# Where the prompt's heads stand in the attention loop, and how a pair's heads are taken out

## The chip, the cores and the metric

The kernel runs on one core of one Trainium2 chip. The metric is device time in microseconds (us) of one execution of the whole program, a decoder step of four layers. The attention of layer 2 is one stage of it, and the change is in that stage alone.

## What is computed

Layer 2 is stick-breaking attention with 16 heads of 64, over two kinds of rows: a prompt of 272 rows, and 8 sequences of 4 new rows each, with 1024 earlier keys and values per sequence that lie in pages of 128 in a pool.

```python
z = jnp.einsum('bqhd,bshd->bhqs', qblk, kf) * scale + bf
mask = (k_pos[None, :] < pblk[:, None])[None, None]
log_not = jnp.where(mask, jax.nn.log_sigmoid(-z), 0.0)
between = lax.cumsum(log_not, axis=3, reverse=True) - log_not
wts = jnp.where(mask, jnp.exp(jax.nn.log_sigmoid(z) + between), 0.0)
return jnp.einsum('bhqs,bshd->bqhd', wts, vf)
...
mp = op.reshape(bp, lp, D_MODEL) @ attn_w_o[j]
ms = os_.reshape(bs, ls, D_MODEL) @ attn_w_o[j]
```

Both results go through one output projection with `attn_w_o`, prompt rows and sequence rows side by side (304 columns).

## The kernel before

The 8 sequences are worked in 4 pairs `p`, and the pages of a pair in slots: slot `sl` holds 4 key pages, or 4 value pages. One loop over `u` (L1562 on) does a quarter of a slot a step:

- `keys_t(u+2)` turns 8 blocks of 128x128 of the key pages round on TensorE (L1332), and ScalarE and VectorE copy them out (L1337, L1338);
- `keys(u)` multiplies them with the queries into the scores `zs` (L1351): 4 matmuls, each on its own 32 columns of the array;
- `values(u-24)`, every second step, multiplies two value pages with the weights into `av` (L1415): 4 matmuls, again each on its own 32 columns, two for each page; the first of a pair also takes the new rows (L1413);
- `scores`, `weights` and `weights_t` make a pair's weights in between, and `heads(p)` (L1424 on) turns a pair's finished `av` round (L1428), then takes the heads out, ScalarE the rounded part into `ohi` (L1443) and VectorE the rest into `olo` (L1444).

Key steps run up to `u` = 63, value steps from `u` = 24 to `u` = 86, so the steps after 63 have values alone.

The prompt's own attention is cut into pieces of two heads: `prompt_z` (scores, L1477 and L1478), `prompt_c` (running sums, L1491 to L1495) and `prompt_o` (times the values, L1506 to L1508), in the order z1, o0, c1, z2 and so on, 23 pieces within the loop. The table `at` names the step `u` behind which each one is written.

A page is loaded by one DMA of 512 KB that SyncE issues into one of 13 buffers (8 `raw`, 5 `rawx`), in a fixed order: key and value pages in turn, then the 8 blocks of `attn_w_o`. A load waits until the page that held the buffer is used up (`key_done`). Blocks of `attn_w_o` are then split into a rounded part (`hi`, L208, ScalarE) and a rest (`lo`, L211, VectorE).

The code is not run in the order in which it is written: the framework that builds the program sets one fixed order for each engine beforehand, by times of its own, and each engine then works strictly through its list. The lists are what is compared below.

Of the kernel before, what the change touches and what calls it, by code (L numbers as in the profile page):

```python
# [9 lines left out]
F32 = mybir.dt.float32  # L10
F32R = mybir.dt.float32r
I32 = mybir.dt.int32
AF = mybir.ActivationFunctionType
ALU = mybir.AluOpType
# [46 lines left out]
class Trunk:  # L61
# [1211 lines left out]
    def attention(self, l):  # L1273
        nc, I, O = self.nc, self.I, self.O
        v = nc.vector
        with self.tc.tile_pool(name="att", bufs=1) as ap:
# [146 lines left out]
            def heads(p):  # L1423

                am = va.pop(p)
                po = self.bank()
                for c in range(4):
                    nc.tensor.transpose(po[:, c * 128:(c + 1) * 128], am[:, c * 128:(c + 1) * 128], self.ident)  # L1428
                cs = slice(NP + 8 * p, NP + 8 * p + 8)
                for h in range(2):  # L1430
                    hs = slice(h * 64, h * 64 + 64)
                    for i in range(2):

                        o = 32 * i + 4 * h
                        for c0, c1 in ((0, 3), (3, 4)):
                            if c0 == 0:
                                pv = po[hs, o:o + 408].rearrange("p (c x) -> p c x", x=136)[:, :, 0:128].rearrange("p c (s x) -> p c s x", x=64)[:, :, :, 0:4]
                            else:

                                pv = po[hs, 384:512].rearrange("p (s x) -> p s x", x=64)[:, :, 24 + o:28 + o].unsqueeze(1)  # L1440
                            hi = ohi[hs, 4 * i + c0:4 * i + c1, cs].rearrange("p c (s q) -> p c s q", q=4)
                            lo = olo[hs, 4 * i + c0:4 * i + c1, cs].rearrange("p c (s q) -> p c s q", q=4)
                            nc.scalar.activation(hi, pv, AF.Copy)  # L1443
                            v.tensor_tensor(lo, pv, hi.bitcast(F32), ALU.subtract)  # L1444

            z2 = ap.tile([80, 16, 16], F32, name="z2")[64:80]
            L2 = ap.tile([80, 16, 16], F32, name="L2")[64:80]
# [117 lines left out]
            ohi = self.up.tile([128, ND, N], F32R, tag="uhi", name="ohi")  # L1565
            olo = self.up.tile([128, ND, N], F32R, tag="ulo", name="olo")
            prompt = [(f, d - lag) for d in range(10) for f, lag in ((prompt_o, 2), (prompt_c, 1), (prompt_z, 0)) if 0 <= d - lag < 8]

            at = [22 + k * 2 for k in range(23)]
            del prompt[0]  # L1570
            for u in range(4 * (16 + LAG) + 3):
                if u + LEAD < 64:
                    keys_t(u + LEAD)
                if u < 64:
                    keys(u)
                p, r = divmod(u, 16)
                if p < 4:
                    if r == 8:
                        scores(p, 0)
                    if r == 10 and p < 3:  # L1580
                        queries(p + 1)
                if 0 < p < 5:
                    if r == 0:
                        scores(p - 1, 1)
                        weights(p - 1)
                    if r == 5:
                        weights_t(p - 1)
                c = u - 4 * LAG
                if c >= 16 and c % 16 == 1:
                    heads(c // 16 - 1)  # L1590
                if 0 <= c < 64:
                    values(c)
                if u == 4 * (16 + LAG) - 6:
                    self.split_blocks(self.index[("o", l), 0, 1])
                while at and at[0] == u:
                    f, d = prompt.pop(0)
                    f(d)
                    del at[0]
# [117 lines left out]
```

## Time and profile before

| what | us |
|---|---|
| median of 3 runs | 1662.12 (1660.5 to 1664.52) |
| profiled execution | 1663.34 |
| its span | 1661.6 |
| TensorE busy | 1510.3 |
| VectorE busy | 1206.0 |
| ScalarE busy | 829.3 |
| GpSimd busy | 546.8 |

Times in the rows are counted from the start of the span. The loop of the attention lies between about 780 and 993 us. In a row of the timeline the first number is the start and the second how long the group took from first start to last end; since matmuls overlap, what a group costs is read from its start to the start of the next. A multiplication of 32-bit numbers runs as two passes, so a row of the built order is two in the trace (`x8` in the trace is `x4` in the order); the transposes are one.

### The profile page before, as it was taken

To read this page: it belongs to the slowest core of one execution; us is meant where nothing else is said; L and a number is where in the kernel's file an instruction comes from. 1 tells how busy PE (TensorE), PEld (TensorE's weight loads), DVE (VectorE), ACT (ScalarE), POOL (GpSimd) and SP (SyncE) were. 2 spreads that over 40 slices of the span, in tenths; PEclk is the share of its full clock that TensorE was granted. 3 is DMA by queue.
4 is the path that set the end of the run, shared out by engine and by line. 5 is a ranking of instruction groups with operands and counts; after the bars stand their busy time and mean duration, and the time that the engine had idled before them with its cause. 6 is when DMAs were issued, how large, how long until landed. Compare 5 with 4: busy or idle time off the path is not lost.

```text
span 1661.6 us, 31539 instructions
## 1 busy us (share of the span) xinstructions
PE 1510.3 (91%) x11336; PEld 1391.7 (84%) x11336; DVE 1206.0 (73%) x2513; ACT 829.3 (50%) x1483; POOL 546.8 (33%) x986
## 2 busy tenths in 40 slices
PE   3487999999899999999999988999978578999997
PEld 3376999999789999998665538999978478999997
DVE  6977589985689985644554545989877895699953
ACT  5453466654366563434444434665535333666643
POOL 7945045532265541101000000555283342144400
PEclk9978999999999999999999998999989698999999
DMA  6113455565325554564887796455524113455551
GB/s 114 15 46 120 145 153 160 153 188 164 102 90 163 161 160 150 164 216 142 300 304 273 281 372 175 148 163 158 167 83 127 32 34 94 140 168 171 156 169 47
DMA packets 220960, 256.24 MB, mean 154 GB/s; under 512 B 59045, under 2 KB 171861, under 8 KB 220720
## 3 DMA queue, kind: packets, MB, share of 16 engines
q1 hardware_dynamic: 218292, 249.15, 48.3%
q0 software_dynamic: 2368, 5.08, 0.9%
q8 instruction: 89, 1.46, 0.4%
q14 instruction: 67, 0.55, 0.1%
q10 hardware_dynamic: 144, 0.01, 0.0%
HBM read 246.78 MB, written 6.43 MB: 152 GB/s over the span
## 4 chain that ended last, share of the span: by engine, by line
PE 61%; DVE 8%; POOL 2%; issue 1%; DMA 1%; ACT 1%; SPq 0%; DVEq 0%; POOLq 0%; ACTq 0%
PE bk L248 16%; PE bk L250 16%; PE bk L249 16%; PE bk L1332 4%; PE zs L1351 2%; PE av L1415 2%; DVE lo L211 1%; DVE t L1102 1%; DVE E L1111 1%; PE bk L1491 1%; PE bk L1506 1%; DMA raw<-in_attn_w_o 1%; DVE t L1101 1%; DVE s L648 0%; PE bk L1494 0%
## 5 line engine op out<-in xcount | busy, mean ns | idle before, releaser
L208 ACT ACTIVATE hi<-raw 128x1024 fp32r<-128x1024 f32 x328 | 344.0, 1056 | 283.8 <-PE bk L249 234.7
L248 PE MATMUL bk<-uhi,hi 128*128 128x304 f32 (+1 forms) x1600 | 478.1, 303 | 7.6 <-ACT uhi L374 7.6
L249 PE MATMUL bk<-ulo,hi 128*128 128x304 f32 (+1 forms) x1600 | 482.7, 302 | 1.8 <-DVE ulo L375 1.8
L250 PE MATMUL bk<-uhi,lo 128*128 128x304 f32 (+1 forms) x1600 | 483.1, 303 | 0.0
L211 DVE TENSOR_TENSOR lo<-raw,hi 128x1024 fp32r<-128x1024 f32 x304 | 374.5, 1237 | 140.3 <-ACT hi L208 138.9
L248 PEld LDWEIGHTS bk<-uhi,hi 128*128 128x128 f32 x1600 | 300.1, 189 | 9.4 <-ACT uhi L374 8.8
L249 PEld LDWEIGHTS bk<-ulo,hi 128*128 128x128 f32 x1600 | 302.4, 189 | 3.7 <-DVE ulo L375 3.2
L250 PEld LDWEIGHTS bk<-uhi,lo 128*128 128x128 f32 x1600 | 301.8, 189 | 1.2 <-issue 0.6
L248 PE MATMUL bk<-ghi,hi 128*128 128x304 f32 (+1 forms) x704 | 212.7, 302 | 3.9 <-DVE so L531 3.2
L249 PE MATMUL bk<-glo,hi 128*128 128x304 f32 (+1 forms) x704 | 212.0, 301 | 0.0
L250 PE MATMUL bk<-ghi,lo 128*128 128x304 f32 (+1 forms) x704 | 210.8, 301 | 0.0
L467 ACT ACTIVATE c<-hx,cpT 128x320 f32<-128x320 f32 (+1 forms) x176 | 113.0, 645 | 94.0 <-DVE hx L461 92.8
L211 POOL TENSOR_TENSOR lo<-raw,hi 128x1024 fp32r<-128x1024 f32 x24 | 58.0, 2415 | 291.5 <-ACT hi L208 247.5
L459 POOL COPY hx<-stT 128x16 f32<-128x16 f32 x176 | 91.0, 522 | 159.1 <-DVE c L469 155.0
L248 PEld LDWEIGHTS bk<-ghi,hi 128*128 128x128 f32 x704 | 132.6, 188 | 5.4 <-DVE so L531 4.3
L249 PEld LDWEIGHTS bk<-glo,hi 128*128 128x128 f32 x704 | 132.7, 188 | 0.1
L250 PEld LDWEIGHTS bk<-ghi,lo 128*128 128x128 f32 x704 | 132.4, 189 | 0.0
L464 POOL COPY hp<-hx 128x2 f32<-128x2 f32 x176 | 94.6, 537 | 105.2 <-DVE hx L460 98.5
L460 DVE TENSOR_TENSOR hx<-bk,rstd 128x272 f32<-128x272 f32 (+1 forms) x176 | 76.1, 433 | 31.2 <-PE bk L250 26.1
L469 DVE SCALAR_TENSOR_TENSOR c<-hx,cpT,c 128x320 f32<-128x320 f32 (+1 forms) x176 | 94.8, 540 | 1.1
L468 DVE SCALAR_TENSOR_TENSOR c<-hx,cpT,c 128x320 f32<-128x320 f32 (+1 forms) x176 | 94.6, 540 | 0.8 <-ACT c L467 0.7
L249 PE MATMUL bk<-zlo,hi 128*128 128x304 f32 (+1 forms) x256 | 77.6, 306 | 3.6 <-DVE zlo L1167 3.6
(488 smaller groups left out, 2698.8 us busy)
## 6 DMA issues: line engine op xcount, KB each, us to landing
raw<-in_ffn_w_up SPq DMA_DIRECT2D x352, 256.0 KB
raw<-in_ffn_w_down SPq DMA_DIRECT2D x88, 512.0 KB
raw<-in_cache_v SPq DMA_DIRECT2D x46, 512.0 KB
raw<-in_cache_k SPq DMA_DIRECT2D x34, 512.0 KB
raw<-in_ssm_w_glu SPq DMA_DIRECT2D x64, 256.0 KB
rawx<-in_cache_k SPq DMA_DIRECT2D x30, 512.0 KB
raw<-in_attn_w_qkv SPq DMA_DIRECT2D x24, 512.0 KB
rawx<-in_cache_v SPq DMA_DIRECT2D x18, 512.0 KB
```

Of the source, the lines that this page charges most:

```text
L208: nc.scalar.activation(hi, raw, AF.Copy)
L211: eng.tensor_tensor(lo, raw, hi.bitcast(F32), ALU.subtract)
L248: mm(out, whi, ahi, start=start, stop=False)
L249: mm(out, whi, alo, start=False, stop=False)
L250: mm(out, wlo, ahi, start=False, stop=stop)
L459: nc.gpsimd.tensor_copy(hv[:, :, 0:2], stT[:, ft].rearrange("p (b t) -> p b t", t=2))
L460: nc.vector.tensor_tensor(h[:, 2 + t0:2 + NP], ps[:, t0:NP], self.rstd[:, t0:NP], ALU.mult)
L464: nc.gpsimd.tensor_copy(hp[:, ft], h[:, NP:NP + 2])
L467: nc.scalar.activation(o, h[:, 2 + t1:], AF.Identity, bias=par(3, ft), scale=par(2, ft))
L468: nc.vector.scalar_tensor_tensor(o, h[:, 1 + t1:HEXT - 1], par(1, ft), o, ALU.mult, ALU.add)
L469: nc.vector.scalar_tensor_tensor(o, h[:, t1:HEXT - 2], par(0, ft), o, ALU.mult, ALU.add)
L1332: nc.tensor.transpose(pt[:, r * 256 + g * 128:r * 256 + (g + 1) * 128], raw[2 * s + g][:, d * 128:(d + 1) * 128], self.ident)
```

## The change

The table of steps is stretched: the 23 pieces stood behind the steps 22, 24, ... 66, and stand behind 26, 28, 31, 34, ... 84 now. In `heads`, the four blocks of a pair are turned round into a bank 120 columns apart and not 128: each block overwrites the last 8 columns of the one ahead of it, which hold nothing that is taken, and the wanted columns of all four blocks then lie at one even distance. So one operation takes what two took (3 blocks and 1 block before): 4 on ScalarE and 4 on VectorE for a pair, where there were 8 and 8.

```diff
                 for c in range(4):
-                    nc.tensor.transpose(po[:, c * 128:(c + 1) * 128], am[:, c * 128:(c + 1) * 128], self.ident)
+                    nc.tensor.transpose(po[:, c * 120:c * 120 + 128], am[:, c * 128:(c + 1) * 128], self.ident)
...
-                        o = 32 * i + 4 * h
-                        for c0, c1 in ((0, 3), (3, 4)):
-                            if c0 == 0:
-                                pv = po[hs, o:o + 408].rearrange("p (c x) -> p c x", x=136)[:, :, 0:128].rearrange("p c (s x) -> p c s x", x=64)[:, :, :, 0:4]
-                            else:
...
-                            nc.scalar.activation(hi, pv, AF.Copy)
-                            v.tensor_tensor(lo, pv, hi.bitcast(F32), ALU.subtract)
+                        pv = po[hs].rearrange("p (c s i z) -> p c s i z", s=2, i=2, z=32)[:, :, :, i, 4 * h:4 * h + 4]
+                        hi = ohi[hs, 4 * i:4 * i + 4, cs].rearrange("p c (s q) -> p c s q", q=4)
+                        lo = olo[hs, 4 * i:4 * i + 4, cs].rearrange("p c (s q) -> p c s q", q=4)
+                        nc.scalar.activation(hi, pv, AF.Copy)
+                        v.tensor_tensor(lo, pv, hi.bitcast(F32), ALU.subtract)
...
-            at = [22 + k * 2 for k in range(23)]
+            at = [26 + k * 8 // 3 for k in range(23)]
```

With the new table the built order changes in the whole loop, and nowhere behind the loop but for two loads of `ffn_w_up` that SyncE issues seven places later. Lines from L1429 on have other numbers in the changed kernel (`heads`' transposes L1429 for L1428, its copies L1438 for L1443, pieces of the prompt 5 lines less).

TensorE, end of the loop, before: the last value pages of the last pair, up to the last transposes of `heads`.

```order
L1415 MATMUL av<-raw,wT 32x512 x2
L1415 MATMUL av<-rawx,wT 32x512 x2
L1415 MATMUL av<-raw,wT 32x512 x6
L1415 MATMUL av<-rawx,wT 32x512 x2
L1415 MATMUL av<-raw,wT 32x512 x2
L1415 MATMUL av<-rawx,wT 32x512 x2
L1415 MATMUL av<-raw,wT 32x512 x2
L1428 MATMUL bk<-ident,am 128x128 x4
```

The same place now, with the last piece of the prompt (`prompt_o`, here L1501 to L1503) in it:

```order
L1415 MATMUL av<-raw,wT 32x512 x4
L1501 MATMUL bk<-zp,vp 64x272
L1502 MATMUL bk<-zp,vp 64x144
L1503 MATMUL bk<-z_8018,vx 64x16
L1415 MATMUL av<-raw,wT 32x512 x2
L1501 MATMUL bk<-zp,vp 64x272
L1502 MATMUL bk<-zp,vp 64x144
L1503 MATMUL bk<-z_8018,vx 64x16
L1415 MATMUL av<-rawx,wT 32x512 x2
L1415 MATMUL av<-raw,wT 32x512 x2
L1415 MATMUL av<-rawx,wT 32x512 x2
L1415 MATMUL av<-raw,wT 32x512 x2
```

Before, 28 value matmuls stood in one unbroken row here; now pieces of the prompt stand among them, also between the two pages of one step.

TensorE, the last slots with keys, before: one step with transposes, scores and values.

```order
L1332 MATMUL bk<-ident,raw 128x128 x4
L1332 MATMUL bk<-ident,rawx 128x128 x4
L1351 MATMUL zs<-kt,qb_8015 32x256 x8
L1415 MATMUL av<-raw,wT 32x512 x2
L1415 MATMUL av<-rawx,wT 32x512 x2
```

A place among the last slots with keys now:

```order
L1415 MATMUL av<-raw,wT 32x512 x2
L1332 MATMUL bk<-ident,raw 128x128
L1332 MATMUL bk<-ident,rawx 128x128
L1332 MATMUL bk<-ident,raw 128x128 x4
L1351 MATMUL zs<-kt,qb_8015 32x256
L1332 MATMUL bk<-ident,rawx 128x128 x9
L1415 MATMUL av<-raw,wT 32x512 x2
L1332 MATMUL bk<-ident,rawx 128x128
L1351 MATMUL zs<-kt,qb_8015 32x256
```

Groups of four that stood together are cut into twos and ones, with full-width transposes between them. Counted over the whole list of TensorE, a run being matmuls of one line with nothing else between:

| stretch of the list | line | runs before: length x count | runs now |
|---|---|---|---|
| values begin, to last key transposes | L1351 `zs` | 1x2, 2x3, 4x36, 8x1 | 1x9, 2x24, 3x1, 4x22, 6x1, 8x1 |
| values begin, to last key transposes | L1415 and L1413 `av` | 1x2, 2x11, 4x10, 8x3 | 2x29, 4x4, 6x1, 8x1 |
| last key transposes to the projection | L1351 `zs` | 2x2, 8x1 | 2x2, 6x1 |
| last key transposes to the projection | L1415 and L1413 `av` | 1, 4, 4, 8, 11, 28 | 2x12, 4x1, 6x2, 8x2 |

The prompt's pieces behind the last key transposes were one c and two o; now they are three c, two z and four o.

ScalarE, the end of the loop, before: the copy of the last `av` (`am`), splits of the projection's weights (`hi`), and the heads of the last pair.

```order
L1421 ACTIVATE am<-av 128x512
L208 ACTIVATE hi<-raw 128x1024
L1443 ACTIVATE ohi<-bk 64x3x8
L208 ACTIVATE hi<-raw 128x1024
L1443 ACTIVATE ohi<-bk 64x8
L208 ACTIVATE hi<-raw 128x1024
L1443 ACTIVATE ohi<-bk 64x3x8
L208 ACTIVATE hi<-raw 128x1024
L1443 ACTIVATE ohi<-bk 64x8
L1443 ACTIVATE ohi<-bk 64x3x8
```

The same place now:

```order
L1421 ACTIVATE am<-av 128x512
L208 ACTIVATE hi<-raw 128x1024
L1438 ACTIVATE ohi<-bk 64x4x8
L208 ACTIVATE hi<-raw 128x1024
L1438 ACTIVATE ohi<-bk 64x4x8
L208 ACTIVATE hi<-raw 128x1024
L1438 ACTIVATE ohi<-bk 64x4x8
L208 ACTIVATE hi<-raw 128x1024
L1438 ACTIVATE ohi<-bk 64x4x8
```

The first rows of both halves of the heads are complete with the third operation now, where they were with the fifth.

## Rows read from the trace of the kernel before

**Rows 1.** The page, the span in 40 slices: busy tenths of TensorE and DMA.
```profile
PE   3487999999899999999999988999978578999997
...
DMA  6113455565325554564887796455524113455551
```

**Rows 2.** Windows of the loop and behind it: busy us (instructions), granted clock, DMA share, GB/s.
```profile
818.00:962.08 144.08, 144.08 (x1220) 86.70 (x1223) 74.89 (x138) 62.25 (x124) 0.83 (x4) 1.00 0.79 282
962.08:993.46 31.38, 28.81 (x198) 11.59 (x197) 11.28 (x24) 11.01 (x25) 0.00 (x0) 1.00 1.00 376
993.46:999.26 5.80, 0.00 (x0) 0.00 (x0) 5.26 (x13) 3.87 (x9) 0.00 (x0) 0.68 1.05 386
999.26:1005.00 5.74, 5.74 (x31) 5.74 (x32) 0.69 (x4) 1.34 (x4) 0.00 (x0) 0.73 0.83 215
```

**Rows 3.** Timeline of TensorE: start, us, operation; a full value run and the prompt's pieces.
```profile
830.41 0.74 PE L1477 MATMUL bk<-qT,kT 64*128 64x272 f32 x4
...
831.33 0.66 PE L1332 MATMUL bk<-ident,raw 128*128 128x128 f32 x4
...
832.35 0.64 PE L1351 MATMUL zs<-kt,qb 128*32 128x256 f32 x8
832.92 0.33 PE L1332 MATMUL bk<-ident,rawx 128*128 128x128 f32 x1
...
834.40 1.04 PE L1415 MATMUL av<-raw,wT 128*32 128x512 f32 x8
835.37 0.67 PE L1506 MATMUL bk<-zp,vp 128*64 128x272 f32 x2
...
837.49 0.33 PE L1332 MATMUL bk<-ident,rawx 128*128 128x128 f32 x1
...
863.57 0.73 PE L1491 MATMUL bk<-Lp,tri 128*128 128x272 f32 x2
...
865.56 0.66 PE L1332 MATMUL bk<-ident,raw 128*128 128x128 f32 x4
```

**Rows 4.** Timeline of TensorE: runs of values and scores that were cut short.
```profile
801.31 0.62 PE L1351 MATMUL zs<-kt,qb 128*32 128x256 f32 x4
801.87 0.33 PE L1332 MATMUL bk<-ident,raw 128*128 128x128 f32 x1
...
875.79 1.04 PE L1415 MATMUL av<-raw,wT 128*32 128x512 f32 x2
876.76 0.66 PE L1332 MATMUL bk<-ident,rawx 128*128 128x128 f32 x4
...
878.93 1.05 PE L1415 MATMUL av<-raw,wT 128*32 128x512 f32 x4
879.91 0.46 PE L1507 MATMUL bk<-zp,vp 128*64 128x144 f32 x2
...
965.99 0.65 PE L1351 MATMUL zs<-kt,qb 128*32 128x256 f32 x8
...
968.26 0.73 PE L1491 MATMUL bk<-Lp,tri 128*128 128x272 f32 x2
```

**Rows 5.** Waits, 780 to 1030 us: who waited for whom, us in total, times, longest.
```profile
PEld av L1415 <- DMA raw<-in_cache_v: 2.9, 3, 1.2
PEld av L1415 <- DMA rawx<-in_cache_v: 2.3, 2, 1.1
```

**Rows 6.** Timeline of TensorE at the loop's end: start, us, operation [idle before, releaser].
```profile
979.11 1.06 PE L1413 MATMUL av<-vx,wn 32*32 32x512 f32 x8 [0.86 <-DVE wn L1394]
...
992.80 0.66 PE L1428 MATMUL bk<-ident,am 128*128 128x128 f32 x4 [0.76 <-ACT am L1421]
999.26 1.38 PE L248 MATMUL bk<-ohi,hi 128*128 128x304 f32 x4 [5.81 <-ACT ohi L1443]
```

**Rows 7.** Timeline of ScalarE at the loop's end.
```profile
996.53 0.18 ACT L1443 ACTIVATE ohi<-bk 64x24 fp32r<-64x24 f32 x1
...
999.03 0.19 ACT L1443 ACTIVATE ohi<-bk 64x24 fp32r<-64x24 f32 x1 [1.04 <-DVE olo L1444]
```

More of the change, by code (lines that the diff above doesn't have):

```diff
@@ L1432, in heads @@
                     for i in range(2):
-                        o = 32 * i + 4 * h
-                        for c0, c1 in ((0, 3), (3, 4)):
-                            if c0 == 0:
-                                pv = po[hs, o:o + 408].rearrange("p (c x) -> p c x", x=136)[:, :, 0:128].rearrange("p c (s x) -> p c s x", x=64)[:, :, :, 0:4]
-                            else:
-                                pv = po[hs, 384:512].rearrange("p (s x) -> p s x", x=64)[:, :, 24 + o:28 + o].unsqueeze(1)
-                            hi = ohi[hs, 4 * i + c0:4 * i + c1, cs].rearrange("p c (s q) -> p c s q", q=4)
-                            lo = olo[hs, 4 * i + c0:4 * i + c1, cs].rearrange("p c (s q) -> p c s q", q=4)
-                            nc.scalar.activation(hi, pv, AF.Copy)
-                            v.tensor_tensor(lo, pv, hi.bitcast(F32), ALU.subtract)
+                        pv = po[hs].rearrange("p (c s i z) -> p c s i z", s=2, i=2, z=32)[:, :, :, i, 4 * h:4 * h + 4]
[3 more added lines that the diff above has]
+                        v.tensor_tensor(lo, pv, hi.bitcast(F32), ALU.subtract)
             z2 = ap.tile([80, 16, 16], F32, name="z2")[64:80]
```

## The prediction

> **What bounds the kernel now.** I read the page's slices first, then windows over the loop, then TensorE's timeline row by row, and last the waits. The slices show TensorE at 9 tenths nearly throughout and dented in two slices behind the middle, while DMA goes to its highest [rows 1]: that is the end of the attention loop. The windows cut it in two [rows 2]. From 818 us, where the values begin, to 962.08, where the last key block is turned round, TensorE is busy for 144.08 of 144.08 us, and DMA idles for a fifth: TensorE bounds this **key stretch**. From there to the last transposes of `heads` at 993.46 (the **tail**, 31.38 us) DMA has a share of 1.00 and TensorE waits: 2.9 + 2.3 us for value pages [rows 5] and 0.9 us for a weights copy [rows 6], 6.1 us together. So the tail's TensorE work is 31.4 - 6.1 = 25.3 us. Behind it TensorE stands still for 5.8 us until ScalarE has brought out the last heads [rows 6], and then runs 5.74 us at a mean granted clock of 0.73 [rows 2].
>
> The intended gain is visible in this: pieces of the prompt that leave a stretch where TensorE is full and go where it waits cost nothing, up to 6.1 us.
>
> **What moves.** By the two tables, six pieces leave the key stretch for the tail: two z, two c, two o. A z is 831.33 - 830.41 = 0.92 us, an o 837.49 - 835.37 = 2.12, and half a c 865.56 - 863.57 = 1.99, so a c is 3.98 [rows 3]. Together 2 x (0.92 + 2.12 + 3.98) = 14.0 us.
>
> **What the new order adds.** The built order cuts the runs of values and scores into shorter ones, and here lies the whole forecast. Values are four matmuls on four separate 32-column parts of the array. A run of all four takes 835.37 - 834.40 = 0.97 us from its start to the next operation [rows 3]. A run of two takes 879.91 - 878.93 = 0.98, and a run of a single one 876.76 - 875.79 = 0.97 [rows 4]. So a run costs 0.97 us for each four begun, and one cut in two costs twice. For the scores, half a run takes 801.87 - 801.31 = 0.56 us [rows 4] and a whole one 832.92 - 832.35 = 0.57 [rows 3]; I use 0.56 for each four begun.
>
> The pair at 878.93 stood between two halves of an o, which itself uses only 64 columns, and yet nothing ran beside it: 0.98 us [rows 4]. Three pairs stand so in the new tail; ran they beside the o, 3 x 0.97 = 2.9 us would fall away, and this I keep as the lower end of the tail.
>
> The Trainium skill, TensorEngine Tiling, Key Properties, says that tiles work independently and in parallel, but that a change of the tiling mode drains the engine. By the first half alone those pairs would be free, by the second they are paid in full; the trace agrees with the second.
>
> From the counts of runs in the two orders:
>
> Key stretch. Values: 29 fours begun before (2 + 11 + 10 + 2 x 3), 37 now (29 + 4 + 2 + 2), 8 x 0.97 = +7.8 us. Scores: 43 before (2 + 3 + 36 + 2), 60 now (9 + 24 + 1 + 22 + 2 + 2), 17 x 0.56 = +9.5 us. Less the 14.0 us of pieces that is +3.3. Against it, short runs of both kinds in turn flow into each other: at 965.99, two scores, one value, two scores, four values took 2.27 us to 968.26 [rows 4], where four separate runs would be 2 x 0.56 + 2 x 0.97 = 3.06. The new order has five more such places, up to 5 x 0.8 = 4.0 us back. Bounds -0.7 and +3.3; I take **+1**, in the middle, as both ends come from rows of equal standing. So the key stretch, where the gain should come from, does not get shorter. DMA, idle for a fifth of it, does not end it either way.
>
> Tail. Work before 25.3; pieces +14.0; values 15 fours begun before (1 + 1 + 1 + 2 + 3 + 7), 21 now (12 + 1 + 4 + 4), 6 x 0.97 = +5.8; the place at 965.99 is no longer of that kind, +0.8. That makes 45.9 us, where the tail lasted 31.4: **+14.5**. DMA needed 31.4 us for the tail's loads; it has 45.9, so it is hidden, and what is late next is TensorE itself. The 0.9 us wait for the weights copy goes too, as an o now stands ahead of it. No row shows whether new waits come in for the softplus of the last pieces; bounds 0 and +2. I take 0, since between a z and its c stand an o and at least two value runs, 2.1 + 1.9 us of other work.
>
> **Heads.** In the key stretch the 8 + 8 operations of a pair stand on engines that are half idle (62 and 75 of 144 us [rows 2]); their halving is worth nothing there. Only the last pair counts. The projection's first matmul needs one i of both halves h. That was the fifth operation, at 999.03, and is the third now, in the place of the one at 996.53 [rows 7]: **-2.5 us**. The splits of the projection's weights still stand between them on ScalarE, one of which must also land; its loads are earlier than before. Bounds -1 and -3. The transposes 120 columns apart are the same four matmuls.
>
> **Clock.** In the 5.74 us behind the wait the granted clock was 0.73, a loss of 0.27 x 5.74 = 1.55 us against full speed [rows 2]. The wait will be 3.3 instead of 5.8 us and stand behind a full engine. Bounds -1.55 and 0, I take **-0.8**.
>
> Behind the loop the order is the same but for two weight loads issued a little later, beside plenty of others; zero.
>
> **Sum.** +1 + 14.5 - 2.5 - 0.8 = +12.2 us. On the profiled execution, 1663.34 + 12.2 = 1675.5; this one lies 1.2 above the median of the runs, so 1674.3 by the median, **1674**.
>
> **Rivals.**
> 1. *The cuts are free* (faster). If a cut run fitted beside its neighbours, only the moved pieces would count: the key stretch 14 us shorter, the tail's 6.1 us of waits filled, -6.1 - 2.5 - 0.8 = -9.4, or 1662.1 - 9.4 = 1653. For it: the place at 965.99. Against it: three rows of cut runs at full price, and that TensorE had no gap in the key stretch though 13 value runs there were already cut. This is what decides: the cuts cost 15 + 5.8 + 0.8 = 21.6 us in my sum, and the change loses as soon as they cost more than 9.4, that is 44% of it.
> 2. *The cuts cost half* (no change). -9.4 + 10.8 = +1.4, 1663.5. It needs many more places of the kind of 965.99 than I count.
> 3. *Worse still.* The last pair's weights or a piece's softplus come late and TensorE waits in the tail, where its strict order lets nothing by: +2 to +8 on top, 1676 to 1682. For it: the 0.86 us wait [rows 6] shows the kind. Against it: every such chain has more work ahead of it now than before.
>
> **Chances.** Forecast 0.66 (its own range 1668 to 1681, from the bounds: least -0.7 + 14.5 - 2.9 - 3 - 1.55 = +6.4, most +3.3 + 16.5 - 1 = +18.8), worse still 0.10, half price 0.12, free 0.12. A difference of about 0.2% (3.3 us) is what a measurement can tell from none. Faster 0.12, same 0.12, slower 0.76. The range 1662 to 1682 holds the forecast, the half price and most of the third; it leaves out the free cuts and the ends.
>
> **What would show it.** Right: the last key transposes again near 962 us, within 3; value runs of two at 0.97; the last transposes of `heads` near 1008; no DMA wait in the tail; the first projection matmul 3.3 us behind them, not 5.8; the projection at a higher granted clock. Wrong: last key transposes near 948 (the cuts are free), or waits of TensorE for ScalarE or VectorE of several us in the tail (worse). If the loop ends as forecast and the time does not, something behind the loop gives it back, most likely the loads of `ffn_w_up`, which have more time now.

## The result, and the profile after

| | before | after |
|---|---|---|
| median, us | 1661.74 (1659.35 to 1664.52) | 1677.37 (1673.93 to 1681.58) |
| profiled execution | 1663.34 | 1677.37 |
| its span | 1661.6 | 1675.7 |

The change is slower: ratio 1.0092, interval [1.0078, 1.0106]. Windows of the changed kernel, cut at the same places of its list as [rows 2]: the key stretch, the tail, the wait before the projection, and 5.74 us behind it (columns as there):

```profile
816.95:960.97 144.02, 144.02 (x1142) 79.39 (x1142) 66.06 (x115) 56.77 (x106) 1.02 (x4) 1.00 0.80 282
960.97:1009.43 48.46, 47.74 (x274) 21.83 (x273) 18.34 (x34) 14.88 (x31) 0.00 (x0) 1.00 0.78 269
1009.43:1012.66 3.23, 0.00 (x0) 0.00 (x1) 2.98 (x9) 2.61 (x7) 0.00 (x0) 0.70 0.91 333
1012.66:1018.40 5.74, 5.74 (x24) 5.55 (x25) 2.53 (x4) 1.22 (x2) 0.00 (x0) 0.57 0.93 178
```

The span is 14.1 us longer: -1.05 ahead of the key stretch, -0.06 in it (144.02 for 144.08), **+17.08 in the tail** (48.46 for 31.38), -2.57 in the wait (3.23 for 5.80), +0.70 behind. The key stretch has given six pieces away and is no shorter; the tail has taken them in and shows its DMA share at 0.78, not 1.00.

The page, 40 slices, TensorE (compare [rows 1]): the dent in slice 24 has gone (9 for 8); slice 25, where the wait before the projection lies now, is still at 8; and the program is longer.

```profile
PE   3487999999899999999999998999979588999998
```

TensorE's timeline of the changed kernel (start, us, operation) shows runs cut in two, as in [rows 4], now all over the loop. In the tail, two value matmuls (`x4`) between two parts of an o, and four in two pairs, each pair between other pieces:

```profile
962.38 0.67 PE L1501 MATMUL bk<-zp,vp 128*64 128x272 f32 x2
962.98 1.05 PE L1415 MATMUL av<-rawx,wT 128*32 128x512 f32 x4
963.97 0.46 PE L1502 MATMUL bk<-zp,vp 128*64 128x144 f32 x2
...
994.18 1.05 PE L1415 MATMUL av<-raw,wT 128*32 128x512 f32 x4
995.16 0.67 PE L1501 MATMUL bk<-zp,vp 128*64 128x272 f32 x2
...
1002.03 1.06 PE L1415 MATMUL av<-raw,wT 128*32 128x512 f32 x8
1003.02 0.67 PE L1501 MATMUL bk<-zp,vp 128*64 128x272 f32 x2
```

From its start to the next start each run takes 0.98 or 0.99 us, the pairs at 962.98 and 994.18 as much as the whole run at 1002.03.

Timelines of the changed kernel at the end of the loop, ScalarE's answering [rows 7], and TensorE's last transposes and first projection matmul, answering [rows 6]:

```profile
1009.56 0.18 ACT L1438 ACTIVATE ohi<-bk 64x32 fp32r<-64x32 f32 x1
1009.64 1.05 ACT L208 ACTIVATE hi<-raw 128x1024 fp32r<-128x1024 f32 x1
1011.18 0.19 ACT L1438 ACTIVATE ohi<-bk 64x32 fp32r<-64x32 f32 x1 [0.50 <-DVE olo L1439]
1011.27 1.04 ACT L208 ACTIVATE hi<-raw 128x1024 fp32r<-128x1024 f32 x1
1012.41 0.19 ACT L1438 ACTIVATE ohi<-bk 64x32 fp32r<-64x32 f32 x1
```

```profile
1008.77 0.66 PE L1429 MATMUL bk<-ident,am 128*128 128x128 f32 x4 [0.72 <-ACT am L1421]
1012.66 1.38 PE L248 MATMUL bk<-ohi,hi 128*128 128x304 f32 x4 [3.23 <-ACT ohi L1438]
```

The projection starts behind the third operation of the heads. Each of the three takes 0.2 us, but splits of weights (`hi`, 1.05 us) stand between them.

### The profile page after: what moved, and what is told of

Same layout as the page of the kernel before. It is cut to its first block, busy times and chain, and to the rows that moved or that the text cites. A ratio compares the mean times of both kernels' runs of the same rounds, so it can differ in the third digit from the quotient of the medians.

```text
span 1675.7 us, 31514 instructions
## 1 busy us (share of the span) xinstructions
PE 1528.6 (91%) x11336; PEld 1395.0 (83%) x11336; DVE 1205.5 (72%) x2497; ACT 826.4 (49%) x1467; POOL 542.1 (32%) x986
## 4 chain that ended last, share of the span: by engine, by line
PE 63%; DVE 8%; POOL 1%; issue 1%; ACT 1%; DVEq 0%; ACTq 0%; POOLq 0%
PE bk L249 16%; PE bk L250 16%; PE bk L248 16%; PE bk L1332 4%; PE av L1415 3%; PE zs L1351 3%; DVE lo L211 1%; DVE t L1102 1%; DVE E L1111 1%; PE bk L1486 1%; DVE s L648 1%; PE bk L1501 1%; DVE t L1101 1%; PE bk L1489 0%; PE bk L1472 0%
```

## The experiments

The theory: the moved pieces do pay, but the new order cuts runs of values and scores, and a run costs the same whether it is whole or half. The rival: the pieces were hidden anyway, or the order costs something else, and the cuts cost little.

**The two halves of the change alone.** heads_only keeps the old table:

```diff
-                    nc.tensor.transpose(po[:, c * 128:(c + 1) * 128], am[:, c * 128:(c + 1) * 128], self.ident)
+                    nc.tensor.transpose(po[:, c * 120:c * 120 + 128], am[:, c * 128:(c + 1) * 128], self.ident)
...
-                        for c0, c1 in ((0, 3), (3, 4)):
...
+                        pv = po[hs].rearrange("p (c s i z) -> p c s i z", s=2, i=2, z=32)[:, :, :, i, 4 * h:4 * h + 4]
```

> The new heads alone, with the old table of steps; TensorE's list is as before but for one place. If the cut runs are the cause (theory), the key stretch stays at 144 us and the tail at 31 us, and the wait of the output projection for the last heads falls from 5.8 to about 3.3 us: 2 to 3 us faster than before, about 1659. If the blocks turned round 120 columns apart are the cause (rival), the tail is longer than 31 us and the time at or above 1662.

Measured: 1659.07 us, ratio 0.997 [0.9952, 0.9987]. Windows of heads_only: tail, wait.

```profile
959.35:991.57 32.22, 29.36 (x198) 11.53 (x197) 10.66 (x20) 10.35 (x21) 0.00 (x0) 1.00 0.97 369
991.57:994.92 3.35, 0.00 (x1) 0.01 (x1) 3.05 (x9) 2.64 (x7) 0.00 (x0) 0.81 1.05 387
```

The wait is 3.35 us for 5.80. The new heads alone are a small gain. The tail is 0.84 us longer than before, as the rival would have it, but that lies in the value matmuls (19.43 us for 18.58, from start to start), some of which wait for pages here too; the transposes 120 columns apart do not take longer.

spread_only has the new table and the old heads:

```diff
-            at = [22 + k * 2 for k in range(23)]
+            at = [26 + k * 8 // 3 for k in range(23)]
```

> The new table of steps alone, with the old heads. Theory (cut runs): tail about 48 us as in the changed kernel, wait for the last heads 5.8 us again, so 2 to 3 us slower than the changed kernel, about 1680. Rival (the new heads cost the time): tail near 31 us, 1662 to 1665.

Measured: 1676.52 us, ratio 1.0077 [1.0046, 1.0108]. Windows of spread_only: key stretch, tail, wait.

```profile
816.70:960.91 144.21, 144.21 (x1143) 79.37 (x1147) 67.33 (x123) 58.12 (x114) 1.02 (x4) 1.00 0.79 281
960.91:1009.41 48.50, 47.78 (x273) 22.23 (x273) 18.90 (x38) 15.49 (x35) 0.00 (x0) 1.00 0.78 270
1009.41:1015.10 5.69, 0.00 (x0) 0.00 (x0) 5.18 (x13) 3.86 (x9) 0.00 (x0) 0.66 0.81 242
```

The key stretch and the longer tail are those of the changed kernel, so the loss is the table's. The heads shorten the wait by 2.46 us here too; the medians of the two kernels, measured on two chips, don't resolve that.

**The same tables without cuts.** In spread_whole (new table, new heads) and old_whole (old table, new heads) every step's matmuls are put on TensorE's list behind the last matmul of the step written ahead, so that no run is cut. The work is the same.

```diff
+            def turn(f, *x):
+                n0 = len(nc.cur_bb.bb.instructions)
+                with self.tc.issue_after(last[0]) if last[0] is not None else nullcontext():
+                    f(*x)
+                pe = [i for i in nc.cur_bb.bb.instructions[n0:] if i.engine == nc.tensor.engine]
+                last[0] = pe[-1] if pe else last[0]
...
-                    keys_t(u + LEAD)
+                    turn(keys_t, u + LEAD)
...
-                    values(c)
+                    turn(values, c)
```

> The changed kernel with each step's matmuls queued behind those of the step written ahead of it, so that no run of values or scores is cut: in its list all value runs are fours, eights or more. Theory (cuts cost): TensorE's work is 123 us in the key stretch and 39 us in the tail by the prices of the prediction (0.97 and 0.56 us a run). DMA was busy for 114 us of the key stretch, so it may come near to ending that; key stretch 123 to 131 us, tail 39 to 42, 1650 to 1658. Rival (the pieces lose by their place, waiting for softplus in the tail, or by any cost that is not a cut): no gain on the changed kernel, 1672 to 1680.

> As before, with the old table of steps and the new heads, and the same queueing, so that the runs that the kernel before cut stand whole too. Theory: key stretch 137 us instead of 144, tail still held by DMA at about 31 us, wait for heads 3.3: 8 to 11 us faster than before, 1651 to 1654. Rival: no more than the new heads alone bring, 1659.

Measured: spread_whole 1646.13 us, ratio 0.9899 [0.9869, 0.993]; old_whole 1651.98, ratio 0.9927 [0.9901, 0.9952]. Windows, key stretch and tail, of spread_whole:

```profile
810.90:933.76 122.86, 122.09 (x1140) 75.49 (x1143) 64.27 (x112) 53.31 (x102) 1.02 (x4) 1.00 0.90 329
933.76:974.02 40.26, 39.54 (x278) 20.98 (x277) 19.64 (x38) 16.73 (x35) 0.00 (x0) 1.00 0.93 341
```

and of old_whole:

```profile
816.70:952.48 135.78, 135.22 (x1220) 85.76 (x1223) 72.80 (x130) 60.32 (x116) 0.82 (x4) 1.00 0.83 298
952.48:983.62 31.14, 28.24 (x198) 11.19 (x197) 10.66 (x20) 10.27 (x21) 0.00 (x0) 1.00 1.00 375
```

The changed kernel's loop is 192.5 us long (144.02 + 48.46), that of spread_whole 163.1. Between the two whole kernels the table alone takes 12.9 us from the key stretch and adds 9.1 to the tail: 3.8 us gained. (The prediction counted 6.1 us of waits to fill; TensorE itself was idle for 2.9 us of old_whole's tail, 31.14 less 28.24. The account of the tail below says why the two differ.) So the stretched table does what it was to do, once the runs stay whole. old_whole came as expected. spread_whole's two stretches did too, but its time lies 4 us below the expected 1650: that range left room for DMA to end the key stretch, and with a share of 0.90 it did not.

**The cut by itself.** The order of spread_whole differs from that of the changed kernel in more than the cuts. cut_pages is spread_whole with one cut put back by hand: a step's first value page ahead of its key transposes and scores, the second behind them (`values` takes the page as a second argument).

```diff
             for u in range(4 * (16 + LAG) + 3):
+                c = u - 4 * LAG
+                if 0 <= c < 64:
+                    turn(values, c, 0)
...
-                    turn(values, c)
+                    turn(values, c, 1)
```

> The changed table and heads with the whole runs of spread_whole, and one cut put in by hand: a step's first value page stands ahead of its key transposes and scores, its second page behind them, so a run of four value matmuls becomes two runs of two with other TensorE work between. The work is the same. By the counts of the built list 16 more value runs are begun in the key stretch (38 fours begun, 22 in spread_whole) and 1 more in the tail. Theory (a run costs 0.97 us whether it has two or four matmuls): key stretch 122.9 + 16 x 0.97 = 138.4 us (137 to 140), tail 40.3 + 1 = 41.2, the whole 1646.1 + 16.5 = 1662.6, ratio to before near 1.000. Rival (a cut costs little, spread_whole gained by something else in its order): key stretch under 128 us, the whole under 1652, ratio under 0.994.

Measured: 1670.23 us, ratio 1.0035 [1.0019, 1.005], where spread_whole, run again beside it, has 0.9895. Windows of cut_pages (key stretch, tail), the key stretch of spread_whole_2, and the timeline of cut_pages at cut steps:

```profile
815.28:957.64 142.36, 141.80 (x1140) 78.63 (x1143) 64.33 (x112) 54.59 (x102) 1.02 (x4) 1.00 0.79 284
957.64:999.86 42.22, 41.50 (x278) 21.29 (x277) 19.65 (x38) 16.77 (x35) 0.00 (x0) 1.00 0.89 325
```

```profile
812.89:936.08 123.19, 122.20 (x1140) 75.49 (x1143) 64.30 (x112) 53.37 (x102) 1.02 (x4) 1.00 0.90 329
```

```profile
820.58 1.05 PE L1417 MATMUL av<-vx,wn 32*32 32x512 f32 x4
821.56 1.05 PE L1419 MATMUL av<-raw,wT 128*32 128x512 f32 x4
822.54 0.66 PE L1332 MATMUL bk<-ident,raw 128*128 128x128 f32 x4
...
842.52 1.03 PE L1419 MATMUL av<-raw,wT 128*32 128x512 f32 x4
843.48 0.33 PE L1332 MATMUL bk<-ident,rawx 128*128 128x128 f32 x1
```

The rival falls: half a run at 842.52 costs 0.96 us. The key stretch is 19.2 us longer than that of the run beside it (142.36 for 123.19) and the tail 2.0. My number was too low, 16 + 1 runs, and the rows at 820.58 say why. Where the new rows of a pair come in (L1417), a cut leaves two matmuls on the new rows and two on the page, both on the same two 32-column parts. I had counted such four as one run; they take two turns, 0.98 us each. Counted by turns in the trace, the key stretch has 22 more (19 steps cut, three of them beginnings of pairs with one turn more) and the tail two, both at the beginning of the last pair, which took 3.92 us (973.99 to 977.91) for 1.99 in spread_whole: 24 in all. The time of the values, from start to start, rose by 22.0 us (58.5 for 36.5 in key stretch and tail), 0.92 a turn; scores and key transposes took 0.9 less. The 20th cut step costs nothing that shows: the last step with keys has no key transposes, only scores between its halves, and from the last key transpose to the next o it took 2.32 us (957.57 to 959.89) for 2.29 in spread_whole. So what makes a cut dear is work other than scores between the halves; the place at 907.48, shown below, says the same. By the medians cut_pages is 24.6 us slower than the run beside it, 21.1 of which lie in the two stretches; where the other 3.5 come from these runs don't show.

**The same order again, and the heads with nothing between.** spread_whole_2 is spread_whole unchanged.

> spread_whole once more, beside the two others of this call. As before: key stretch 122.9 us within 1, tail 40.3, wait 3.2, ratio 0.990 within 0.003.

Measured: 1645.64 us, ratio 0.9895 [0.9876, 0.9914]. heads_first is spread_whole with the first weight block's split ahead of the prompt's last `ohi`, and all later ones behind the last heads:

```diff
+                o_late = self.plan[i][0][0][0] == "o" and self.o_done
...
+                with self.tc.issue_after(self.o_done[0]) if o_late else self.tc.issue_after(self.behind_act.ins) if self.behind and self.plan[i][0][:2] == (("glu", 0), 0) else nullcontext():
...
+                with self.tc.issue_after(self.o_split[0]) if d == 7 else nullcontext():
+                    self.o_last = nc.scalar.activation(ohi[:, d, :NP], po[:, :NP], AF.Copy).ins
...
-                    nc.scalar.activation(va[p], av, AF.Copy)
+                    with self.tc.issue_after(self.o_last) if p == 3 else nullcontext():
+                        nc.scalar.activation(va[p], av, AF.Copy)
...
+                if p == 3:
+                    self.o_done = (hi_op.ins, lo_op.ins)
...
-                    self.split_blocks(self.index[("o", l), 0, 1])
+                    self.split_blocks(self.index[("o", l), 0, 0])
```

> spread_whole, with ScalarE's and VectorE's lists changed at the end of the loop: the split of the projection's first weight block (hi, lo) stands ahead of the prompt's last heads, all later splits behind the last pair's heads, so that nothing stands between the four operations of the heads on either engine. TensorE's list in the loop is the same. In spread_whole's trace the heads of the pair ahead, undisturbed, follow each other at 0.45 us (923.24 to 923.69), those of the last pair at 1.2 to 1.6 us with splits between. Theory (the splits between the heads are what is left of the wait): the third operation begins 0.9 us behind the first instead of 2.85, the wait before the projection is 1.3 us instead of 3.23, the whole 1.9 us less, ratio near 0.989. Rival 1 (the first block's split, moved ahead, waits for its load and holds up the copy of av): the wait is 3 us or more, time as spread_whole or longer. Rival 2 (the wait goes, but the projection waits for the later splits or has a lower clock for longer): wait 1.3 us, and the first 5.7 us of the projection or what follows lose 1 to 2 us, time as spread_whole.

Measured: 1645.88 us, ratio 0.9888 [0.987, 0.9906]. Windows of spread_whole_2: wait, whole projection, first matmuls of the next stage.

```profile
976.34:979.57 3.23, 0.00 (x0) 0.00 (x1) 2.98 (x9) 2.62 (x7) 0.00 (x0) 0.73 0.56 201
979.57:1008.90 29.33, 29.32 (x192) 28.89 (x192) 15.59 (x23) 11.08 (x16) 0.00 (x0) 0.91 0.74 170
...
1010.69:1020.00 9.31, 8.65 (x48) 8.27 (x49) 6.17 (x11) 5.72 (x10) 0.00 (x0) 0.82 0.40 115
```

The same three of heads_first:

```profile
979.10:980.30 1.20, 0.00 (x0) 0.00 (x0) 0.47 (x7) 0.57 (x3) 0.00 (x0) 1.00 0.63 208
980.30:1007.24 26.94, 26.93 (x192) 26.69 (x192) 16.84 (x24) 12.99 (x18) 0.00 (x0) 1.00 0.84 200
...
1009.03:1019.70 10.67, 10.00 (x48) 9.62 (x49) 6.17 (x11) 5.71 (x10) 0.00 (x0) 0.68 0.37 107
```

The wait falls to 1.20 us as the theory said, and the clock is not lowered at all in the projection, which takes 26.94 us for 29.33: 2.03 + 2.39 = 4.4 us at this place. The medians show none of it. In these two traces 1.4 us go again in the first 48 matmuls of the next stage, where the clock is 0.68 for 0.82, and 1.5 in a stretch of the following layer: from 1212.70 to 1252.00 in spread_whole_2 39.30 us at a clock of 0.95, the same stretch in heads_first, from 1212.40 to 1253.20, 40.80 us at 0.89.

That is rival 2 in other places, and the 1.5 us that would be left are less than these medians can tell apart. Whether the loss behind the projection belongs to the change of order or to the single execution, one trace of each can't say. heads_first and spread_whole are the fastest here, about 1% below the kernel before.

## Why the prediction was right, and where its sizes were off

The span grew by 14.1 us where +12.2 was forecast. Single terms lie further off: the tail is 2.6 us above its forecast and the clock 1.7, the key stretch 1.1 below, and the key stretch began 1.05 us earlier, which was so at the loop's first matmul already and is not the change's doing. That the sum is off by 1.9 us only is in part luck.

**What bounds the kernel; the six pieces.** Right. The key stretch was full before and is full after, and the tail has no wait for value pages any more: with 48.46 us for its loads DMA is hidden.

**The price of a run.** Right, and the step that carries everything: rows of the changed kernel (0.98 us for a pair), and cut_pages, where nothing but the cut differs in the work. It also holds for pairs between the halves of an o: none ran beside it (962.98), so the lower end that I kept for the tail was not needed. No run cuts the scores alone: their price rests on the rows and on the table below.

**Key stretch: +1 forecast, -0.06 measured.** The sum of it, from the timelines, each operation counted from its start to the next start:

| us | before | after | change | forecast |
|---|---|---|---|---|
| values | 27.99 | 31.89 | +3.9 | +7.8 |
| scores | 20.93 | 28.42 | +7.5 | +9.5 |
| pieces of the prompt | 47.46 | 33.55 | -13.9 | -14.0 |
| key transposes | 41.02 | 43.15 | +2.1 | none |

Values and scores cost 5.9 us less than the price list, more than the 4.0 that I allowed for short runs flowing into each other. One such place, a score, two values and a score, from 907.48 to 908.90:

```profile
907.48 0.40 PE L1351 MATMUL zs<-kt,qb 128*32 128x256 f32 x1
907.50 0.62 PE L1415 MATMUL av<-raw,wT 128*32 128x512 f32 x1
907.72 0.38 PE L1351 MATMUL zs<-kt,qb 128*32 128x256 f32 x1
907.94 1.02 PE L1415 MATMUL av<-raw,wT 128*32 128x512 f32 x3
908.38 0.59 PE L1351 MATMUL zs<-kt,qb 128*32 128x256 f32 x2
908.90 0.66 PE L1332 MATMUL bk<-ident,rawx 128*128 128x128 f32 x4
```

Apart they would be 2 x 0.56 + 0.97 = 2.09 us; they took 1.42. Against it stand the key transposes, which my sum left out: cut into ones and twos between the runs they cost 2.1 us more (in spread_whole, where they stand whole, they take 41.2 us). The two errors nearly cancel.

**Tail: +14.5 forecast, +17.1 measured,** above the highest that the prediction allowed for it (+16.5). This is the term that was mis-sized, in two places. First, I priced a moved piece as it stood whole in the key stretch, but in the tail the pieces are cut too. A z with a value run in its middle:

```profile
973.45 0.72 PE L1472 MATMUL bk<-qT,kT 64*128 64x272 f32 x2
974.11 1.05 PE L1415 MATMUL av<-raw,wT 128*32 128x512 f32 x4
...
975.09 0.49 PE L1472 MATMUL bk<-qT,kT 64*128 64x272 f32 x1
...
975.99 1.48 PE L1415 MATMUL av<-raw,wT 128*32 128x512 f32 x10
```

It costs 2.54 - 0.98 = 1.56 us, for 0.92 whole [rows 3]: its two halves use different 64 rows of the array, and apart they no longer overlap. Both z of the tail are cut so, 1.3 us. Three c took 12.1 for 11.9 and four o 8.8 for 8.5, another 0.5.

Second, I took 5.2 us of waits for value pages out of the work of the tail before. The rows that I read [rows 5] count idle time of the weight loads. TensorE itself was idle for 2.57 of the 31.38 us [rows 2], 0.95 of it for pages. From the last 28 value matmuls of the kernel before:

```profile
981.69 1.07 PE L1415 MATMUL av<-raw,wT 128*32 128x512 f32 x8
...
984.72 0.60 PE L1415 MATMUL av<-rawx,wT 128*32 128x512 f32 x2
...
987.12 1.05 PE L1415 MATMUL av<-rawx,wT 128*32 128x512 f32 x4 [0.23 <-DMA rawx<-in_cache_v]
988.40 1.05 PE L1415 MATMUL av<-raw,wT 128*32 128x512 f32 x4 [0.23 <-DMA raw<-in_cache_v]
...
990.99 1.05 PE L1415 MATMUL av<-raw,wT 128*32 128x512 f32 x4 [0.26 <-DMA raw<-in_cache_v]
```

The first 14 of them took 3.03 us (981.69 to 984.72), 0.87 for each four: whole runs in a row take less than the 0.97 of a run with other work behind it. At that pace 28 take about 6.2 us. They took 10.35 (to 992.04), because the last pages came singly, 1.28 us apart, and the two matmuls of each page took a run of their own: a late page cuts a run as the order does. So some 4.1 us were lost to the pages and not 5.2, an estimate from these rows, and the work was about 26.4 us and not 25.3: 1.1. From there the values cost 6.1 more (20.61 now, 18.58 less 4.1 before), where 6.6 was forecast with the place at 965.99: -0.5. Together 1.3 + 0.5 + 1.1 - 0.5 = 2.4 of the 2.6 us. No new wait for a softplus came, as forecast. In spread_whole, with nothing cut, the tail is 40.26 us.

**Heads: -2.5 forecast, -2.57 measured**, and -2.46 between spread_only and the changed kernel. The transposes 120 columns apart take the same 0.66 us.

**Clock: -0.8 forecast, +0.9 measured.** The sign was wrong, and the size outside its bounds (-1.55 and 0). These windows hold the whole projection, of before and of after:

```profile
999.26:1027.59 28.33, 28.32 (x192) 28.08 (x192) 13.75 (x23) 10.37 (x17) 0.00 (x0) 0.95 0.80 187
```

```profile
1012.66:1041.93 29.27, 29.27 (x192) 28.84 (x192) 15.57 (x23) 11.05 (x16) 0.00 (x0) 0.92 0.78 174
```

The wait got shorter and the projection longer. Of the 2.6 us that the heads gave, 0.9 are lost here.

**Rivals.** The free cuts would have had the last key transposes near 948 and the half price near 1663: they ended at 960.97 and 1677. "Worse still" has the time, 1677, but not its mechanism: TensorE waited for no late softplus, the pieces themselves were dearer.

Open is why the framework's own order cuts more runs with the stretched table: its choice was overridden in spread_whole, not examined.

## What to carry to other kernels

When four small matmuls share the array by columns, count turns and not matmuls: a pair costs as much as a four, when other work follows it, so an order that looks like better overlap can eat the whole gain of the move that it came with. Before moving filler work between stages look at what the list then does to its neighbours, and hold the runs together; here that alone turned 0.9% lost into 1% gained. And compare kernels by stretches of the trace that they share: executions with the same lists up to there reached the key stretch up to 5 us apart (at 810.90 us in spread_whole, on another chip at 812.89 in spread_whole_2 and 816.29 in heads_first).

## What the hardware did that I had not expected

The clock behind a short stop of TensorE. Behind the wait of 5.80 us the next 5.74 us had a granted clock of 0.73 [rows 2]; in spread_only, behind 5.69 us, it was 0.74. Behind waits of 3.2 to 3.35 us more of the projection ran at the lower level, 1.2 GHz: the same 5.74 us had 0.57 in the changed kernel, 0.52 in heads_only, 0.50 and 0.56 in spread_whole and spread_whole_2, 0.60 in old_whole. The clock was down within the wait already, in the long one of before (0.68) as in the short one of the changed kernel (0.70). Behind 1.20 us it did not fall in the projection at all (1.00 in heads_first). So a stop cut from 5.8 to 3.2 us gained less than its length, and one cut to 1.2 us more, at that place. cut_pages, with the same wait of 3.23 us, had 0.70 there, so more than the length of the stop decides; what, these runs don't show.
